# Compression matmuls of four weight tiles issued as one run of sixteen, and another pace of the side lanes

## The chip, the core and the metric

The kernel runs on one core of a Trainium2 chip. The metric is the device time of one launch in microseconds. The core's engines work side by side, each through its own queue of instructions in order: TensorE (PE: matmuls, with PEld for its weight loads), VectorE (DVE), ScalarE (ACT), GpSimd (POOL) and SyncE (SP), which here mostly issues DMAs.

## The reference

The reference is a trunk of two equal layers over 256 tokens of width 1024, in float32. A layer has a gated feed-forward block, three kinds of attention side by side whose results are gated and added, a second feed-forward block, and a gated addition of an embedding. The part that matters is the second kind of attention, `nsa_attention`. Its first branch compresses keys and values: windows of 32 tokens, 16 apart, are laid out as one row each, and a small network turns a row into one key or value.

```python
def compress(t, pos, w1, w2):
    c = t.reshape(bsz, n_chunk, B_CMP_STRIDE, B_GROUPS, B_HEAD_DIM)
    blk = jnp.concatenate([c[:, :-1], c[:, 1:]], axis=2) + pos[None, None, :, None, :]
    blk = blk.transpose(0, 1, 3, 2, 4).reshape(bsz, n_cmp, B_GROUPS, B_CMP_LEN * B_HEAD_DIM)
    return jax.nn.gelu(blk @ w1) @ w2
```

There are 15 windows and two groups, so `blk` has 30 rows of 2048, and `w1` is 2048x256, once for keys and once for values. The product `blk @ w1` is what the change is about. Its result goes through `gelu` and `w2` and is attended to by the same queries as the other two branches of `nsa_attention`.

## The kernel before, in words

Large products split each float32 operand into a high and a low part and add three matmuls (`mul3`, lines L265 to L267). Weights come through SP's queue as tiles of 128x1024 into `raw`; ScalarE copies the high part to `wh` (L258), VectorE subtracts it to get the low part `wl` (L253). There are six buffers of `wh` and six of `wl`. A product of 512 columns (`product`) walks the first 128 tokens through eight steps of the inner dimension and the second 128 tokens eight steps later, and calls `flow.tick()` after each three matmuls.

Attention is made of generators, the sides, that are stepped by these ticks. Side a (first attention), c (third) and b (second) share lane 0, one after the other; each has a pace, the steps that it takes for a tick of the main line (`PACE_A`, `PACE_B`, `PACE_C`, 0.8 each). The side `compressed` has lane 1 to itself at a pace of 1.0. The main line runs the projections A0, A1, A2, Ck, Cq, Bk, Bv, Bq, and then the gates and output products of the three branches in the order 0, 2, 1 (`gate` and `br`). Side a starts after A2, c and `compressed` after Bk, b after branch 0. Where a branch needs a side's result, the main line joins it: what is left of the side is stepped through at once.

The program is put in order by a list scheduler as it is built: on each engine it takes, of the instructions whose inputs are there, the one traced first. `tc.high_priority(offset=n)` makes an instruction count as traced n earlier, and `tc.keep_in_program_order` pins one behind the instruction traced before it on its engine. The scores of attention (`scores`, L1008) are written with both: twelve matmuls of 64 rows a group, of which eleven are ahead of other work and pinned to the one before, and the first is not.

The compression (`compressing`) holds its rows in `e` as 16 pieces of the inner dimension (k) for keys and for values (kv). One matmul takes 128 of the inner dimension, the 32 rows as the stationary operand, and 256 columns of `w1`. Each of four kinds, by kv and by k odd or even, writes another strip of 32 partitions of one PSUM bank, `c_ps` (`cmp` in the profile); a later matmul adds the strips. The weights `w1` are eight tiles of 128x1024 a layer (`Whole`, `w` in the profile), each for four matmuls; they are not split, and go by SP's queue straight into a buffer of `wh` or `wl`, in turn (L397). One is queued behind every second tile of the main line from Bv on. For each tile the loop waits until the tile and two queue places after it are fetched, `ready(j, 3)`, and issues its four matmuls (L1202). After the last, VectorE copies the bank to `c_sb` (L1205).

Of the kernel before, what the change touches and what calls it, by code (L numbers as in the profile page):

```python
# [43 lines left out]
LATE_ON = False  # L44
FLIPS = ["flip"]
POINTS = (5, 8, 11, 14, 18, 21)
PACE_A, PACE_B, PACE_C = 0.8, 0.8, 0.8

# [166 lines left out]
def trunk(ctx: ExitStack, tc: tile.TileContext, a: dict, out: bass.AP, index: list):  # L217
    nc = tc.nc
# [7 lines left out]
    def bank(tag, bufs, name):  # L226
        return psum.tile([128, 512], F32, tag=tag, bufs=bufs, name=name)
# [726 lines left out]
    def attention(i, norm, after):  # L954
# [215 lines left out]
        w1 = w2 = None  # L1170
# [10 lines left out]
        def compressing():  # L1181
            pos = pool.tile([128, 2, 2, 8], F32, name="pos")
            nc.sync.dma_start(pos, a["pos"][i].rearrange("p (v s j) -> p v s j", v=2, s=2))
            e = base.tile([128, 2, 2, 8, 32], F32, tag="blk", bufs=6, name="e")
            yield
            nc.vector.memset(e[:, :, 1, :, 31:32], 0.0)
            for kv in range(2):
                for s in range(2):
                    nc.vector.tensor_tensor(
                        e[:, kv, s, :, 0:32 - s],  # L1190
                        half[0][:, 2 * kv:2 * kv + 2, :].rearrange("p g (n j) -> p j (g n)", j=8)[:, :, s:],
                        pos[:, kv, s, :, None].to_broadcast([128, 8, 32 - s]), op=ALU.add)
                yield
            c_ps = bank("tp", 3, "cmp")
            for j in range(8):
                while not w1.ready(j, 3):
                    yield
                w = w1(j)
                for x in range(4):
                    k, kv = 2 * j + x // 2, x % 2  # L1200
                    q = 32 * (2 * (k % 2) + kv)
                    nc.tensor.matmul(c_ps[q:q + 32, :256], e[:, kv, k // 8, k % 8], w[:, 256 * x:256 * x + 256], start=j == 0, stop=j == 7)  # L1202
                yield
            c_sb[0] = pool.tile([128, 256], F32, name="c_sb")
            nc.vector.tensor_copy(c_sb[0], c_ps[:, :256])  # L1205

        def compressed():

            yield from compressing()
            yield  # L1210
            g_ps = tp_bank("gl")[:, :128]
# [320 lines left out]
        w1 = Whole(i, "w1")  # L1532
# [228 lines left out]
```

## Time and profile before

| | us |
|---|---|
| median of 3 runs | 1295.36 |
| lowest and highest | 1295.05 and 1295.36 |
| the profiled execution, time | 1295.46 |
| the profiled execution, span | 1293.7 |
| PE busy | 1283.7 |
| DVE busy | 1069.8 |
| ACT busy | 907.8 |

The span reaches from the first instruction's start to the last one's end; the execution's time has some 1.8 us around it. Attention takes some 250 us of each layer, from about 185 to 440 us in the first. Matmuls overlap in PE's pipeline, so the length of one, or a busy sum, says less than the distance between starts. A matmul of unsplit float32, as in the compression, stands in the profile as two records, and a merged row of the timeline counts records.

### The profile page before, as it was taken

The page shows a single profiled execution, that of the slowest core. Times are in us where ns is not written, and L with a number is a line of the kernel's source. Part 1 is how long each engine was busy: PE and PEld are TensorE (multiplying, and loading weights), DVE is VectorE, ACT ScalarE, POOL GpSimd, SP SyncE. Part 2 cuts the span into 40 slices and gives each one's busy share as a digit, 9 for nine tenths or more (in the row PEclk, how much of TensorE's full clock was granted, in tenths as well). Part 3 has the DMA queues.
Part 4 walks back from the last instruction along what each step waited for, and adds up shares of the span by engine and source line. Part 5 has one row for each costly group of instructions (what it writes and reads, how often), then busy time and mean ns, then how long its engine had stood idle before and what let it go on. Part 6 is the DMA issues. An engine that isn't in the chain of part 4 may idle for free.

```text
span 1293.7 us, 17861 instructions
## 1 busy us (share of the span) xinstructions
PE 1283.7 (99%) x6250; PEld 1052.7 (81%) x6250; DVE 1069.8 (83%) x1736; ACT 907.8 (70%) x1450; POOL 27.5 (2%) x46
## 2 busy tenths in 40 slices
PE   9999999999999999999999999999999999999997
PEld 7888888877878888888888888888778788888886
DVE  7878977666788799997799999777677978999975
ACT  6778667577587487876667876676765866787664
POOL 0000000000000000000000000000000000000000
PEclk9999999999999999999999999999999999999999
DMA  8778788465534568687666787865654435678772
GB/s 320 230 232 269 206 243 224 165 237 167 189 118 129 175 185 244 212 241 214 212 195 237 201 250 229 250 180 200 224 178 144 140 130 194 206 202 240 237 222 83
DMA packets 137179, 263.73 MB, mean 204 GB/s; under 512 B 71670, under 2 KB 77174, under 8 KB 137088
## 3 DMA queue, kind: packets, MB, share of 16 engines
q1 hardware_dynamic: 134128, 252.56, 63.4%
q0 software_dynamic: 2528, 9.47, 2.2%
q8 instruction: 49, 0.80, 0.3%
q10 hardware_dynamic: 432, 0.56, 0.1%
q14 instruction: 42, 0.34, 0.1%
HBM read 245.74 MB, written 1.08 MB: 191 GB/s over the span
## 4 chain that ended last, share of the span: by engine, by line
PE 99%; issue 0%; DVE 0%; ACT 0%; POOLq 0%; POOL 0%; DVEq 0%; ACTq 0%
PE ff L266 8%; PE ff L265 8%; PE ff L267 8%; PE fo L267 5%; PE fo L265 5%; PE fo L266 5%; PE p L265 4%; PE p L267 4%; PE p L266 4%; PE gate L265 4%; PE gate L266 4%; PE gate L267 4%; PE s L1008 2%; PE br L265 2%; PE A L266 2%; PE A L267 2%
## 5 line engine op out<-in xcount | busy, mean ns | idle before, releaser
L253 DVE TENSOR_TENSOR wl<-raw,wh 128x1024 fp32r<-128x1024 f32 (+1 forms) x410 | 491.8, 1213 | 85.2 <-ACT wh L258 84.2
L258 ACT ACTIVATE wh<-raw 128x1024 fp32r<-128x1024 f32 (+1 forms) x410 | 424.7, 1048 | 155.0 <-DMA raw<-in_wst 59.1
L266 PE MATMUL ff<-wl,nT 128*128 128x512 f32 x464 | 180.9, 390 | 0.0
L267 PE MATMUL ff<-wh,nT 128*128 128x512 f32 x464 | 180.3, 390 | 0.0
L265 PE MATMUL ff<-wh,nT 128*128 128x512 f32 x464 | 171.7, 390 | 0.0
L267 PE MATMUL fo<-wh,gT 128*128 128x512 f32 x304 | 117.1, 390 | 0.0
L266 PE MATMUL fo<-wl,gT 128*128 128x512 f32 x304 | 115.7, 389 | 0.0
L265 PE MATMUL fo<-wh,gT 128*128 128x512 f32 x304 | 114.3, 390 | 0.0
L266 PEld LDWEIGHTS ff<-wl,nT 128*128 128x128 f32 x464 | 87.1, 188 | 18.2 <-DVE wl L253 0.3
L265 PEld LDWEIGHTS ff<-wh,nT 128*128 128x128 f32 x464 | 87.1, 188 | 18.0
L267 PEld LDWEIGHTS ff<-wh,nT 128*128 128x128 f32 x464 | 87.1, 188 | 17.9
L265 PE MATMUL gate<-wh,nT 128*128 128x512 f32 x192 | 78.3, 408 | 0.0
L266 PE MATMUL gate<-wl,nT 128*128 128x512 f32 x192 | 76.8, 400 | 0.0
L267 PE MATMUL gate<-wh,nT 128*128 128x512 f32 x192 | 76.8, 402 | 0.0
L267 PEld LDWEIGHTS fo<-wh,gT 128*128 128x128 f32 x304 | 57.1, 188 | 11.8
L266 PEld LDWEIGHTS fo<-wl,gT 128*128 128x128 f32 x304 | 57.1, 188 | 11.8
L265 PEld LDWEIGHTS fo<-wh,gT 128*128 128x128 f32 x304 | 57.1, 188 | 11.7
L1021 ACT ACTIVATE p<-p,st 128x128 f32<-128x128 f32 (+1 forms) x128 | 56.6, 446 | 13.2 <-DVE st L1019 12.1
L606 ACT ACTIVATE whole<-flip 128x1024 uint16<-128x1024 uint16 x32 | 43.0, 1367 | 20.9 <-DMA flip<-cut 20.9
L600 ACT ACTIVATE cut<-gated 128x1024 uint16<-128x1024 uint16 (+1 forms) x48 | 46.3, 974 | 8.6 <-DVE gated L646 8.6
L253 DVE TENSOR_TENSOR wl<-x,wh 128x1024 fp32r<-128x1024 f32 x42 | 50.5, 1224 | 2.0 <-ACT wh L258 2.0
L258 ACT ACTIVATE wh<-x 128x1024 fp32r<-128x1024 f32 x42 | 43.8, 1049 | 5.7 <-DVE x L253 4.5
(391 smaller groups left out, 2734.0 us busy)
## 6 DMA issues: line engine op xcount, KB each, us to landing
raw<-in_wst SPq DMA_DIRECT2D x408, 512.0 KB, 4.4
w<-in_wst SPq DMA_DIRECT2D x16, 512.0 KB, 4.6
y<-in_wst POOLq DMA_DIRECT2D x6, 1024.0 KB, 6.6
band<-table SPq DMA_DIRECT2D x10, 512.0 KB, 4.7
xy<-in_wst POOLq DMA_DIRECT2D x4, 512.0 KB, 4.1
raw<-in_wbv SPq DMA_DIRECT2D x4, 420.0 KB, 3.1
xt<-in_xt SPq DMA_DIRECT2D x4, 256.0 KB, 5.5
raw<-in_wst SPq DMA_DIRECT2D x4, 256.0 KB, 5.2
```

The costliest lines, as they stand in the source:

```text
L253: nc.vector.tensor_tensor(o, x, y, op=ALU.subtract)
L258: nc.scalar.activation(hi, src, AF.Copy)
L265: nc.tensor.matmul(ps, xh, wh, start=start, stop=False, **kw)
L266: nc.tensor.matmul(ps, xh, wl, start=False, stop=False, **kw)
L267: nc.tensor.matmul(ps, xl, wh, start=False, stop=stop, **kw)
L600: nc.scalar.activation(cut.rearrange("p (w n) -> p w n", w=2), halves(src)[:, :128 * m].rearrange("p n w -> p w n"), AF.Copy)
L606: tc.keep_in_program_order(nc.vector.tensor_copy(to, of) if late else nc.scalar.activation(to, of, AF.Copy))
L1008: ins = nc.tensor.matmul(o, q[r, x, qb[m], t * 128:(t + 1) * 128], kk, start=x + y == 0, stop=x == 1)
L1021: nc.scalar.activation(p[j], p[j], AF.Exp, bias=st[:, j:j + 1], scale=-1.0, accum_out=st[:, n + j:n + j + 1])
```

## The change

The loop over eight tiles becomes a loop over two groups of four. It waits until the fourth tile of a group, and two queue places after it, are fetched, and then traces sixteen matmuls in the order of k and kv, so that each four in a row write the four strips. All but the first of a group count as traced 300 earlier and are pinned to the one before, as in `scores`. The terms of the sum are the same. Besides, `PACE_A` goes from 0.8 to 0.75, and `PACE_B` and `PACE_C` from 0.8 to 0.9.

```diff
-PACE_A, PACE_B, PACE_C = 0.8, 0.8, 0.8
+PACE_A, PACE_B, PACE_C = 0.75, 0.9, 0.9
...
             c_ps = bank("tp", 3, "cmp")
-            for j in range(8):
-                while not w1.ready(j, 3):
+            for b in range(0, 8, 4):
+                while not w1.ready(b + 4 - 1, 3):
                     yield
-                w = w1(j)
-                for x in range(4):
-                    k, kv = 2 * j + x // 2, x % 2
-                    q = 32 * (2 * (k % 2) + kv)
-                    nc.tensor.matmul(c_ps[q:q + 32, :256], e[:, kv, k // 8, k % 8], w[:, 256 * x:256 * x + 256], start=j == 0, stop=j == 7)
+                w = [w1(j) for j in range(b, b + 4)]
+                for k in range(2 * b, 2 * b + 2 * 4):
+                    for kv in range(2):
+                        q, o = 32 * (2 * (k % 2) + kv), 256 * (2 * (k % 2) + kv)
+                        with tc.high_priority(offset=300 if (k, kv) != (2 * b, 0) else 0):
+                            ins = nc.tensor.matmul(c_ps[q:q + 32, :256], e[:, kv, k // 8, k % 8], w[k // 2 - b][:, o:o + 256], start=k < 2, stop=k >= 14)
+                        if (k, kv) != (2 * b, 0):
+                            tc.keep_in_program_order(ins)
                 yield
```

## Prediction

> **What bounds the kernel now.** I read the page's busy shares first, then the chain that ended last, then the timeline of TensorE (PE) around the changed matmuls.
>
> ```profile
> span 1293.7 us, 17861 instructions
> PE 1283.7 (99%) x6250; PEld 1052.7 (81%) x6250; DVE 1069.8 (83%) x1736; ACT 907.8 (70%) x1450; POOL 27.5 (2%) x46
> PE 99%; issue 0%; DVE 0%; ACT 0%; POOLq 0%; POOL 0%; DVEq 0%; ACTq 0%
> L253 DVE TENSOR_TENSOR wl<-raw,wh 128x1024 fp32r<-128x1024 f32 (+1 forms) x410 | 491.8, 1213 | 85.2 <-ACT wh L258 84.2
> L258 ACT ACTIVATE wh<-raw 128x1024 fp32r<-128x1024 f32 (+1 forms) x410 | 424.7, 1048 | 155.0 <-DMA raw<-in_wst 59.1
> w<-in_wst SPq DMA_DIRECT2D x16, 512.0 KB, 4.6
> ```
>
> The last-ending chain is PE itself, 99%. Nothing else ends a wait that matters, so what counts is PE's issue time: the distance from one matmul's start to the next one's start. Durations overlap and cannot be added; starts can be subtracted. In the timeline rows below the first column is the start and the second the length of the merged group. A compression matmul is two records, so x2 is one matmul, x26 thirteen.
>
> ```profile
> 282.51 0.38 PE L273 MATMUL yt<-ident,yn 128*128 128x128 f32 x2
> 282.82 1.91 PE L1202 MATMUL cmp<-w,e 128*32 128x256 f32 x26
> 284.67 0.32 PE L1008 MATMUL s<-kC,qC 64*128 64x128 f32 x1
> 284.92 0.64 PE L1202 MATMUL cmp<-w,e 128*32 128x256 f32 x8
> 285.49 0.88 PE L1008 MATMUL s<-kC,qC 64*128 64x128 f32 x11
> 286.30 0.63 PE L1202 MATMUL cmp<-w,e 128*32 128x256 f32 x6
> 286.86 0.50 PE L265 MATMUL gate<-wh,nT 128*128 128x512 f32 x1
> ...
> 288.10 0.39 PE L267 MATMUL gate<-wh,nT 128*128 128x512 f32 x1
> 288.42 0.62 PE L1202 MATMUL cmp<-w,e 128*32 128x256 f32 x2
> 288.97 0.49 PE L265 MATMUL gate<-wh,nT 128*128 128x512 f32 x1
> ...
> 289.39 0.63 PE L1202 MATMUL cmp<-w,e 128*32 128x256 f32 x6
> 289.96 0.50 PE L265 MATMUL gate<-wh,nT 128*128 128x512 f32 x1
> 290.30 0.40 PE L266 MATMUL gate<-wl,nT 128*128 128x512 f32 x1
> ...
> 299.51 0.64 PE L1202 MATMUL cmp<-w,e 128*32 128x256 f32 x8
> 300.08 0.51 PE L1265 MATMUL yc<-pT,vC 128*128 128x512 f32 x1
> ...
> 308.06 0.63 PE L1202 MATMUL cmp<-w,e 128*32 128x256 f32 x6
> 308.62 0.50 PE L265 MATMUL gate<-wh,nT 128*128 128x512 f32 x1
> ...
> 312.71 0.62 PE L1202 MATMUL cmp<-w,e 128*32 128x256 f32 x2
> 313.26 0.50 PE L265 MATMUL gate<-wh,nT 128*128 128x512 f32 x1
> ```
>
> The reader is to see three things. First, the 32 matmuls of a layer run in eight scattered pieces (13, 4, 3, 1, 3, 4, 3, 1). Second, a piece costs the same whether it holds one matmul (288.42 to 288.97: 0.55 us), three (0.57) or four (299.51 to 300.08: 0.57), because four of them write four different 32-column strips and run together; thirteen (282.82 to 284.67) cost 1.85, four such rounds, so each further round costs (1.85-0.55)/3 = 0.43. Third, each piece pays at its borders. Two ordinary rows give the plain step:
>
> ```profile
> 303.63 0.40 PE L266 MATMUL br<-wl,yA 128*128 128x512 f32 x1
> 303.86 0.40 PE L267 MATMUL br<-wh,yA 128*128 128x512 f32 x1
> 304.19 0.98 PE L1008 MATMUL s<-kB,qB 64*128 64x256 f32 x12
> ```
>
> Full matmul to full matmul takes 0.23 us. Full to narrow takes 0.32 (288.10 to 288.42), 0.09 more; the first full matmul after a narrow one takes 0.34 (289.96 to 290.30), 0.11 more. A pair of borders costs 0.20.
>
> **What the compression costs before.** The five pieces after 288 cost 0.55+0.57+0.57+0.56+0.55 = 2.80, and five border pairs 1.00. The three pieces between 282.82 and 286.86 stand among twelve score matmuls, which would have paid the borders themselves. Those twelve alone take, at another place of the layer,
>
> ```profile
> 257.88 0.89 PE L1008 MATMUL s<-kC,qC 64*128 64x128 f32 x12
> 258.70 0.40 PE L265 MATMUL Bv<-wh,nT 128*128 128x280 f32 x1
> ```
>
> 0.82 us, so these three cost 4.04-0.82 = 3.22. Sum: 7.02 us a layer. The compression's busy time on PE is the same in both layers:
>
> ```profile
> 0.00:640.00 640.00, 6.33 (x64) 1.94 (x64) 0.42 (x1) 1.00 0.68 211
> 640.00:1294.00 654.00, 6.33 (x64) 1.94 (x64) 0.42 (x1) 0.99 0.64 197
> ```
>
> so 14.04 us in all.
>
> **The change, part by part.** *Sixteen in one run.* Sixteen matmuls are four full rounds; the piece of thirteen was three full rounds and one with a single matmul, so a whole run costs the same 1.85, and 2.05 with its borders. Two a layer: 4.10, against 7.02: 2.92 less a layer, 5.84 in all. The arithmetic, the weight loads and the copy of the sum out of PSUM are the same in number.
>
> *What keeps it from that.* Fifteen of the sixteen are put ahead of other work and pinned to the one before; the first is not. The scheduler takes a far later instruction when nothing earlier is ready: the row 304.19 is a score group of the second branch's side, which starts only after branch 0, while branch 0 is still in its first `br` product. The new second run is traced after its fourth tile is fetched, but its first matmul needs only tile 4 and can be taken as such a filler; the scattered single at 288.42 shows that place. Then tiles 4 and 5 follow at once (8 matmuls), tile 6 and tile 7 when they land. Tile 7 is issued late:
>
> ```profile
> 297.19 0.46 SPq L397 DMA_DIRECT2D w<-in_wst  x1
> ```
>
> and lands some 4.6 us on (the page's median for `w`), near 301.8. Pieces of 8, 4 and 4 would cost (0.55+0.43)+0.57+0.57+3×0.20 = 2.72 instead of 2.05: 0.67 less gain a layer. The first run has no such break: its tiles were there when thirteen and three of its matmuls ran at 282.82 and 284.92. So the second run's price lies between 2.05 and 2.72 (and, with a loose first matmul, higher still: a rival below). I take the middle, 0.33 a layer lost.
>
> *The score group in the first stretch.* Its first matmul at 284.67 stood apart from its eleven, and the compression sat between. With the compression gone from there a full matmul may take the place:
>
> ```profile
> 360.67 0.38 PE L1008 MATMUL s<-kB,qB 64*128 64x256 f32 x1
> 360.98 0.50 PE L266 MATMUL gate<-wl,nT 128*128 128x512 f32 x1
> 361.87 0.98 PE L1008 MATMUL s<-kB,qB 64*128 64x256 f32 x11
> ```
>
> Such a split costs 0.31 (360.67 to 360.98) and a border pair 0.20, 0.51 a layer; it takes place or not. I put down 0.2.
>
> *Waits and buffers.* No DMA is added; the sixteen `w` loads keep their place in SP's queue, so its order before the next weight loads is the same. The run holds two more `wh` and two more `wl` buffers of six for as long as tile 4 waits for tile 7, at most from 288 to about 312. Behind a late release stand ScalarE's `wh` copies and VectorE's `wl` subtractions for the next products. Cover: a gate product of four tiles gives its first tile free seven steps (21 full matmuls, 4.8 us) before the next product needs that buffer with four left, and copy and subtraction take 1.05 and 1.21 (1048 and 1213 ns in the page's groups). I take nothing; if the cover were gone, each layer would lose up to those 2.3 us. On PE's own queue everything stands behind a run's last four, should tile 7 land later than the scheduler thinks; one microsecond late is one lost, in each layer.
>
> *Pace.* By the code side a now takes a step at 0.75 of the main line's ticks, c and b at 0.9. This adds no instruction. It moves work of VectorE and ScalarE, which is off the path while PE is fed, and decides how many score groups split: seven of fourteen a layer now (rows of L1008 that hold x1; 284.67 and 360.67 are two of the first layer's), at 0.51 each. No row shows the other pace. One group more or less in each of two sides is ±1.0 a layer, ±2.0 in all; all fourteen split or none, ±7, are the far ends. I take zero, since the row gives no direction.
>
> **Sum.** 5.84 - 2×0.33 - 2×0.2 = 4.8 us less. The profiled execution took 1295.46 (span 1293.7), the median is 1295.36, so 1290.6.
>
> **Where the skill prices a piece by itself.** From the rows, a piece between full matmuls costs beside its rounds of 0.43 the border pair of 0.20 and 0.12 of filling inside (0.55-0.43): 0.32. The Trainium skill, TensorEngine Tiling (Array Packing), Key Properties, says that a change of tiling mode drains TensorE, whatever the modes are. The skill's TensorE: Matmul & The Clock Gate, Single matmul latency, puts what streaming hides of a matmul at 398 cycles of 2.4 GHz, 0.166 us; two such a piece, an estimate by that page, are 0.33, and by it six pieces and three rounds fewer a layer would give 3.27, or 1289.9 after my deductions. The trace agrees with it between full matmuls; whether it holds beside score groups is the first rival.
>
> **The rivals.**
>
> *Every piece is as dear (faster than the sum).* My 3.22 for the stretch with the scores holds three pieces, of which two border on scores; if six pieces less a layer brought 0.32 each, with 3 of 11 rounds less (3×0.43), a layer would save 3.21, and 2×3.21-1.06 = 5.4: 1290.0. Against it: the stretch, measured whole, came out at 3.22 with its six rounds (2.58), so its pieces cost 0.21 each. Chance 0.05.
>
> *The runs come apart (about no change).* Each first matmul is taken long before its fifteen (0.55+0.20 = 0.75 for it), and the second run's rest comes as tiles land (7, 4, 4: 2.72). A layer then pays 2.05+0.75+0.75+2.72 = 6.27, and a split score group 0.51: 0.24 saved, 0.5 in all: 1294.9. For it: seven score groups, pinned in the same way, split just so. Against it: the score group's halves write two banks, the compression one bank, whose operands are there at 282.82. Chance 0.11.
>
> *The faster side starves PE (slower).* Place: side b's softmax before the last joins, at pace 0.9. The first two rows are all work, the last two that on the tile `p` alone (PE, PEld, DVE, ACT):
>
> ```profile
> 360.00:380.00 20.00, 20.00 (x113) 15.32 (x112) 18.73 (x59) 16.34 (x46) 0.00 (x0) 1.00 0.50 159
> 380.00:400.00 20.00, 20.00 (x109) 15.61 (x108) 17.12 (x52) 18.58 (x47) 0.00 (x0) 1.00 0.35 106
> 360.00:380.00 20.00, 1.80 (x12) 1.46 (x12) 5.77 (x23) 8.72 (x34) 1.00 0.50 159
> 380.00:400.00 20.00, 3.32 (x20) 2.53 (x20) 5.89 (x18) 8.20 (x28) 1.00 0.35 106
> ```
>
> An eighth more of `p` a microsecond makes VectorE 18.73+0.72 = 19.5 of 20 in the first, ScalarE 18.58+1.03 = 19.6 in the second: just short. From 2.4 us of weight tiles late a layer on, the gain is gone; 3.7 a layer make it slower by 0.2%. With 4 a layer: 1298.6. Against it: the clock stands at 1.00 and PE has no gap in either row. Chance 0.08.
>
> *The pace joins score groups.* Two groups a layer fewer split, and both runs whole: 5.84+2.0, so 1287.5. Chance 0.07.
>
> **How the numbers follow.** My forecast, chance 0.69, runs from whole runs and one split group fewer a layer (1288.5) to pieces of 8, 4, 4 with the score group split and one more split (1295.4-5.84+1.34+1.02+1.02 = 1292.9). Change and no change part at 0.2%, 2.6 us, about what a measurement of this kernel can tell: 1292.8 and 1298.0. Faster: 0.67 of the forecast, 0.05 and 0.07, 0.79; same: 0.02+0.11, 0.13; slower 0.08. The range 1287.0 to 1294.5 leaves out the slower rival, half of the one that comes apart, and a little below.
>
> **What would show it.** Right: `cmp` in the timeline as x32, or as x16 with x8, over about 1.85 us each, four border pairs fewer to full matmuls; PE's chain still 99%. Wrong: groups of x2 before a gate matmul (the loose first); `gate`, `br` or `wo` matmuls that wait for `wl` or `wh`; fewer x12 score groups than seven a layer. If PE's idle time grows near 290 to 312, the held buffers did it; near 360 to 410, the pace.

## The result, and the profile after

The changed kernel takes 1287.54 us (median of four runs, 1286.75 to 1288.41) against 1295.36 before: a ratio of 0.9939, 95% interval 0.9921 to 0.9956. It is faster by 7.8 us, where 4.8 was forecast. The profiled execution took 1288.41, the upper end of its runs.

The page first, in the places that were read before: span, busy shares, and the chain that ended last.

```profile
span 1286.6 us, 17873 instructions
PE 1276.2 (99%) x6250; PEld 1051.1 (82%) x6250; DVE 1068.7 (83%) x1736; ACT 904.5 (70%) x1450; POOL 28.6 (2%) x46
PE 89%; DVE 4%; DMA 3%; ACT 2%; issue 2%; SPq 0%; POOL 0%; POOLq 0%; DVEq 0%; ACTq 0%
```

TensorE executes the same number of matmul records, 6250, and is still busy throughout; the other engines do what they did. The chain now passes through DMA, ScalarE and VectorE for a few per cent, which it did not before. The waits of the weight loads say where; the columns are the sum in us, how often, and the longest.

```profile
PEld ff L265 <- ACT wh L258: 1.2, 2, 0.7
PEld ff L266 <- DVE wl L253: 1.0, 2, 0.6
```

These are in the feed-forward blocks, which the change does not touch. The other runs of this kernel are up to 1.7 us shorter. A second profiled execution of it, of 1287.77 us (Experiment 2), has none of these four waits, and its chain is PE for 98%; it has a wait of another kind, shown in Experiment 5.

The timeline of TensorE around the compression, first layer (start, length of the merged group; two records are one compression matmul):

```profile
289.24 0.38 PE L1008 MATMUL s<-kC,qC 64*128 64x256 f32 x1
289.55 0.50 PE L265 MATMUL br<-wh,yA 128*128 128x512 f32 x1
...
291.12 0.97 PE L1008 MATMUL s<-kC,qC 64*128 64x256 f32 x11
292.03 0.44 PE L273 MATMUL yt<-ident,yn 128*128 128x128 f32 x2
...
294.13 1.93 PE L1203 MATMUL cmp<-w,e 128*32 128x256 f32 x32
295.99 0.55 PE L273 MATMUL pt<-ident,p 128*128 128x128 f32 x3
296.47 0.88 PE L1008 MATMUL s<-kC,qC 64*128 64x128 f32 x12
...
300.40 1.93 PE L1203 MATMUL cmp<-w,e 128*32 128x256 f32 x32
302.26 0.50 PE L1267 MATMUL yc<-pT,vC 128*128 128x512 f32 x1
302.69 0.98 PE L1008 MATMUL s<-kC,qC 64*128 64x256 f32 x12
```

Both runs are whole: 32 records without other work between them, 1.86 us each (294.13 to 295.99, 300.40 to 302.26). The second layer has the same two rows. The score groups at 296.47 and 302.69 are whole as well; only the one at 289.24 still has its first matmul apart. What remains of the compression's busy time on PE, one row a layer (the second column the stretch, the third PE):

```profile
0.00:640.00 640.00, 3.87 (x64) 1.87 (x64) 0.41 (x1) 1.00 0.69 213
640.00:1287.00 647.00, 3.89 (x64) 1.77 (x64) 0.42 (x1) 1.00 0.64 197
```

It was 6.33 a layer. Counted over both layers in the order of TensorE's instructions, the compression's 16 pieces are now 4, the 28 score groups that stood in 42 pieces stand in 36, and the stretches of narrow work between full matmuls are 40 instead of 50.

### The profile page after: what moved, and what is told of

Its sections match the earlier page's. It is cut to its first block, busy times and chain, and to the rows that moved or that the text cites. A ratio compares the mean times of both kernels' runs of the same rounds, so it can differ in the third digit from the quotient of the medians.

```text
span 1286.6 us, 17873 instructions
## 1 busy us (share of the span) xinstructions
PE 1276.2 (99%) x6250; PEld 1051.1 (82%) x6250; DVE 1068.7 (83%) x1736; ACT 904.5 (70%) x1450; POOL 28.6 (2%) x46
## 4 chain that ended last, share of the span: by engine, by line
PE 89%; DVE 4%; DMA 3%; ACT 2%; issue 2%; SPq 0%; POOL 0%; POOLq 0%; DVEq 0%; ACTq 0%
PE ff L266 6%; PE ff L265 6%; PE ff L267 6%; PE fo L267 5%; PE fo L265 5%; PE fo L266 5%; PE gate L266 4%; PE gate L267 3%; PE gate L265 3%; PE p L266 3%; PE p L267 3%; PE p L265 3%; DMA raw<-in_wst 3%; DVE wl L253 2%; PE s L1008 2%; PE br L265 2%
```

## The prices, and what the experiments were to tell apart

Theory "pieces": TensorE is fed all the time, so the time follows from what it has to issue. From the rows: 0.43 us for a round of compression matmuls and 0.12 for each piece, 0.20 for the borders of each narrow stretch; a score piece costs 0.31 with one matmul (289.24 to 289.55) and 0.9 with eleven or twelve (291.12 to 292.03), so 0.19 and about 0.12 for each two. These are scores of 256 columns; a group of 128 columns costs 0.82 (257.88 to 258.70 in the prediction), and the count takes no account of that. By these prices the narrow work of both layers comes to 50.9 us before and 43.0 after, 7.9 less. The rival theory, "pace", gives the runs the 5.8 us that the prediction worked out for whole runs, and the other 2 to the paces of the side lanes. The order of TensorE's instructions is known before a kernel runs, so each expectation is a count at these prices, taken from the 1295.4 before. The kernel before was measured again beside the experiments and came out between 1295.36 and 1295.88; each ratio is to the one on the same chip. "Ranked" below means that an instruction counts as traced earlier (`high_priority`).

| kernel | compression pieces a layer | score pieces, stretches (both layers) | count | measured median | ratio to before, 95% interval |
|---|---|---|---|---|---|
| before | 13, 4, 3, 1, 3, 4, 3, 1 | 42, 50 | | 1295.4 | |
| the change | 16, 16 | 36, 40 | 1287.5 | 1287.54 | 0.9939 (0.9921 to 0.9956) |
| runs alone | 16, 12, 4 | 36, 40 | 1287.5 | 1288.03 | 0.9946 (0.9934 to 0.9959) |
| pace alone | 10, 1, 13, 4, 4 | 42, 46 | 1293.0 | 1292.53 | 0.9980 (0.9971 to 0.9989) |
| runs of four | 12, 12, 4, 4 | 40, 46 | 1290.4 | 1290.27 | 0.9961 (0.9949 to 0.9974) |
| not pinned | 5, 2, 1, 2, 3, 3, 1, 8, 2, 1, 4 | 46, 58 | 1300.4 | 1299.01 | 1.0029 (1.0017 to 1.0040) |
| later bank first | 16, 16 | 34, 38 | 1286.5 | 1286.19 | 0.9924 (0.9911 to 0.9938) |
| one run of 32 | 32 | 42, 44 | 1289.7 | 1288.26 | 0.9942 (0.9930 to 0.9955) |
| first ranked too | 20, 8, 4 | 38, 44 | 1289.2 | 1290.64 | 0.9959 (0.9946 to 0.9971) |
| later bank, pace 1.0 | 16, 16 | 34, 38 | 1286.5 | 1286.70 | 0.9928 (0.9916 to 0.9940) |
| pace of a alone | 16, 16 | 36, 40 | 1287.5 | 1287.94 | 0.9943 (0.9931 to 0.9955) |

## Experiment 1: the runs without the paces, the paces without the runs

The runs alone:

```diff
-PACE_A, PACE_B, PACE_C = 0.75, 0.9, 0.9
+PACE_A, PACE_B, PACE_C = 0.8, 0.8, 0.8
```

> The runs of sixteen with the old paces (0.8 each). Theory 'pieces': the time is set by how many narrow pieces and border pairs TensorE has to issue (0.43 us a compression round, 0.12 a piece, 0.20 a border pair, 0.51 a split score group); the order that this kernel gets has 6 compression pieces and 36 score pieces in 40 narrow stretches, against 16, 42 and 50 before and 4, 36 and 40 with the whole change, so about 7.9 us less than before, 1287.5, the same as the whole change. Rival 'pace': the pace joined the score groups and brought some 2 us of the 7.8; then this kernel saves 5.8 or less, 1289.6 or above.

It took 1288.03. The trace of this kernel, first layer, the rows of L1203 and L1008 from 288 to 308 us:

```profile
288.91 1.93 PE L1203 MATMUL cmp<-w,e 128*32 128x256 f32 x32
291.69 0.98 PE L1008 MATMUL s<-kC,qC 64*128 64x256 f32 x12
296.00 1.50 PE L1203 MATMUL cmp<-w,e 128*32 128x256 f32 x24
304.45 0.64 PE L1203 MATMUL cmp<-w,e 128*32 128x256 f32 x8
305.02 0.62 PE L1008 MATMUL s<-kB,qB 64*128 64x256 f32 x5
306.00 0.62 PE L1008 MATMUL s<-kB,qB 64*128 64x256 f32 x5
307.82 0.38 PE L1008 MATMUL s<-kB,qB 64*128 64x256 f32 x2
```

With the old paces the second run does come apart, into twelve and four, as the prediction had feared; yet the gain is there, because the score pieces are down to 36 here too. So the runs, not the paces, took the score groups from 42 pieces to 36.

The paces alone are the kernel before with only the first line of the change, 0.75, 0.9 and 0.9.

> The old loop by tiles with the new paces. Theory 'pieces': 10 compression pieces and 42 score pieces in 46 stretches, by the same prices 2.4 us less than before, 1293.0; no score group is joined by the pace. Rival 'pace': the side work placed otherwise frees TensorE by itself, some 2 us through joined score groups, or the kernel gets slower where VectorE and ScalarE fill up between 360 and 400 us (1298 or more).

1292.53, 0.998 (0.9971 to 0.9989): the paces by themselves are worth 1.4 to 3.8 us by this interval, but only with the old loop. Its score pieces are 42 still; what the paces change is where the loose compression matmuls fall, 5 pieces a layer instead of 8. With the runs in place that is no longer to be had: the two gains do not add.

## Experiment 2: only side a's pace

```diff
-PACE_A, PACE_B, PACE_C = 0.75, 0.9, 0.9
+PACE_A, PACE_B, PACE_C = 0.75, 0.8, 0.8
```

> The runs of sixteen with only side a's pace changed (0.75, 0.8, 0.8). Theory 'pieces': the order has the same 4 compression pieces, 36 score pieces and 40 stretches as the whole change, so the same time, 1287.5; the paces of b and c bring nothing. Rival 'pace of b and c': they keep VectorE and ScalarE in time for the last join of side b; without them the kernel loses 1 us or more, 1288.5 and up.

> The whole change once more, to stand on the same chip as the two others of this call: 1287.5 by every theory.

1287.94 (1287.79 to 1289.05) beside 1287.77 (1287.03 to 1289.10) for the whole change on the same chip: no difference that can be seen. The paces of b and c bring nothing that shows here. Side a's pace makes the second run whole, but against the runs alone that too shows no difference: 1288.03 with 24 and 8 records.

## Experiment 3: the price of a piece, shorter runs

One tile's four matmuls to a run, ranked and pinned as before:

```diff
-            for b in range(0, 8, 4):
-                while not w1.ready(b + 4 - 1, 3):
+            for b in range(8):
+                while not w1.ready(b, 3):
...
-                w = [w1(j) for j in range(b, b + 4)]
-                for k in range(2 * b, 2 * b + 2 * 4):
+                w = [w1(b)]
+                for k in range(2 * b, 2 * b + 2):
```

> Whole change, but each run holds one tile's four matmuls, eight pinned runs a layer instead of two. Theory 'pieces': the runs stand in 8 pieces (12, 12, 4, 4 a layer) and 40 score pieces in 46 stretches: 5.0 us less than before, 1290.4. Rival 'rounds': the gain is in full rounds of four alone (no single matmuls in a round); these runs are full rounds too, so the whole gain stays, 1287.5.

1290.27, the count's 1290.4. All rounds are full here, and 2.7 us are lost all the same, in borders and in two score groups a layer that stand apart again. Rounds alone are not the gain.

## Experiment 4: sixteen matmuls without rank and pin

```diff
-                        with tc.high_priority(offset=300 if (k, kv) != (2 * b, 0) else 0):
-                            ins = nc.tensor.matmul(c_ps[q:q + 32, :256], ...)
-                        if (k, kv) != (2 * b, 0):
-                            tc.keep_in_program_order(ins)
+                        nc.tensor.matmul(c_ps[q:q + 32, :256], ...)
```

> Whole change without the pins and without the priority: four tiles are still waited for, the sixteen matmuls are free. Theory 'pieces': the order has 22 compression pieces and 46 score pieces in 58 stretches: 5.0 us more than before, 1300.4. Rival 'waiting for four tiles': what helps is that the sixteen are ready at one time; then this kernel keeps most of the gain, 1290 or below.

1299.01: slower than before, 1.0029 (1.0017 to 1.0040). The timeline of this kernel shows what sixteen matmuls that are ready together become when nothing holds them together:

```profile
293.77 1.05 PE L1202 MATMUL cmp<-w,e 128*32 128x256 f32 x10
295.01 0.63 PE L1202 MATMUL cmp<-w,e 128*32 128x256 f32 x4
295.83 0.62 PE L1202 MATMUL cmp<-w,e 128*32 128x256 f32 x2
296.64 0.63 PE L1202 MATMUL cmp<-w,e 128*32 128x256 f32 x4
297.19 0.32 PE L1008 MATMUL s<-kC,qC 64*128 64x128 f32 x1
297.44 0.63 PE L1202 MATMUL cmp<-w,e 128*32 128x256 f32 x6
298.01 0.89 PE L1008 MATMUL s<-kC,qC 64*128 64x128 f32 x11
299.41 0.63 PE L1202 MATMUL cmp<-w,e 128*32 128x256 f32 x6
302.69 0.62 PE L1202 MATMUL cmp<-w,e 128*32 128x256 f32 x2
303.67 1.07 PE L1202 MATMUL cmp<-w,e 128*32 128x256 f32 x16
304.67 0.38 PE L1008 MATMUL s<-kC,qC 64*128 64x256 f32 x1
```

Pieces of one, two and three matmuls at 0.55 to 0.56 each, with other work between them. Beside the paces alone (1292.53), waiting for four tiles without holding them together costs 6.5 us; rank and pin together turn that into a gain. Of the two it should be the rank: with only the pins taken away, the order on TensorE has the same pieces as that of the whole change, and with only the rank taken away nearly those of the kernel here (24 compression pieces in place of 22, and 46 score pieces). This was read from the two orders; neither was run.

## Experiment 5: the first matmul ranked too

```diff
-                        with tc.high_priority(offset=300 if (k, kv) != (2 * b, 0) else 0):
+                        with tc.high_priority(offset=300):
```

> Whole change, but the first matmul of each run counts as traced earlier too. Theory of the prediction ('loose first'): the first matmul at ordinary rank is what can come away from its run, so ranking it with the rest changes nothing or helps, 1287.5 or less. Theory 'pieces' by the order it gets: ranked early, a run starts before its later tiles are there and breaks as they land, 6 pieces (20, 8, 4 a layer) and 38 score pieces in 44 stretches, 6.2 us less than before, 1289.2.

1290.64: the loose first matmul is not the weakness that the prediction took it for. Left at ordinary rank it holds the run back until its last tile is nearly there. Ranked early, its first four matmuls follow the first run at once, the next eight come behind a few transposes, and the last four stand in PE's queue before tile 7 has landed:

```profile
293.80 2.37 PE L1203 MATMUL cmp<-w,e 128*32 128x256 f32 x40
...
296.68 1.07 PE L1203 MATMUL cmp<-w,e 128*32 128x256 f32 x16
...
300.24 0.40 PE L265 MATMUL br<-wh,yA 128*128 128x512 f32 x1
301.92 0.64 PE L1203 MATMUL cmp<-w,e 128*32 128x256 f32 x8 [1.28 <-DMA w<-in_wst]
```

The bracket is the idle time of PE before the row and what ended it: 1.28 us for the DMA of the tile. In the second layer the same wait is shorter:

```profile
936.26 0.64 PE L1203 MATMUL cmp<-w,e 128*32 128x256 f32 x8 [0.60 <-DMA w<-in_wst]
```

The count, 1289.2, has no waits in it; with these two it is 1291.1, half a microsecond above the median. The execution that shows them took 1289.80, though, 1.3 less than that, so the waits need not be what lifts the median over its count. In the changed kernel the same transfer is late as well, by less. In its first profiled execution PE does not wait for it, and the compression's weight loads do for a moment, in both layers together (us, times):

```profile
  DMA w<-in_wst: 0.5, 2
```

In its second profiled execution TensorE itself stands idle before the last four matmuls of the second run, 0.8 us over both layers:

```profile
302.07 0.64 PE L1203 MATMUL cmp<-w,e 128*32 128x256 f32 x8 [0.59 <-DMA w<-in_wst]
935.45 0.64 PE L1203 MATMUL cmp<-w,e 128*32 128x256 f32 x8 [0.21 <-DMA w<-in_wst]
```

Tile 7 was issued at 294.52 there and landed 7.5 us later, at 302.0; the prediction had taken the median of all tiles, 4.6. In the first execution this transfer took 6.6 us.

## Experiment 6: one run of thirty-two, and the buffers

```diff
-            for b in range(0, 8, 4):
-                while not w1.ready(b + 4 - 1, 3):
+            for b in range(0, 8, 8):
+                while not w1.ready(b + 8 - 1, 3):
...
-                w = [w1(j) for j in range(b, b + 4)]
-                for k in range(2 * b, 2 * b + 2 * 4):
+                w = [w1(j) for j in range(b, b + 8)]
+                for k in range(2 * b, 2 * b + 2 * 8):
```

> Whole change with one run of thirty-two a layer instead of two of sixteen: all eight tiles are held until it starts, four of six buffers of each kind. Theory 'pieces': 2 compression pieces, but 42 score pieces in 44 stretches, 5.7 us less than before, 1289.7, if the buffers have cover. Rival 'buffers': with two buffers left of each kind the weight copies come late and TensorE waits inside the gate products, several us a layer: 1295 or more, with gate matmuls waiting for wl in the waits.

1288.26, no slower than the count and 1.4 better, and not to be told from the whole change by the intervals of the table. The run is whole, and no gate product waits:

```profile
319.08 0.39 PE L1268 MATMUL yc<-pT,vC 128*128 128x512 f32 x1
319.40 3.66 PE L1203 MATMUL cmp<-w,e 128*32 128x256 f32 x64
322.99 0.50 PE L265 MATMUL br<-wh,yA 128*128 128x512 f32 x1
```

Four of six buffers of each kind are held until 319 us, and TensorE does not pay for it: in the first layer's attention no weight load waits for `wl` or `wh` but one each before a score group, 0.4 us, about what a weight load into a narrow stretch shows where it waited for nothing. So the prediction's nothing for two held buffers had cover to spare. The run saves a piece and loses it again, since the score groups fall to 42 pieces. The 1.4 us by which the count is too high are not settled; the profiled execution, the slowest of its five, took 1289.33, only 0.4 less than the count.

## Experiment 7: score groups that begin with the later bank

The score groups that still split cost 0.51 each. If a group's first matmul finds its PSUM bank free while the others wait for the group's second bank, beginning with the second should join it:

```diff
-                    for par in range(2):
+                    for par in (1, 0):
...
-                        with tc.high_priority(offset=0 if (m, x, y, par) == (0, 0, 0, 0) else 300):
+                        with tc.high_priority(offset=0 if (m, x, y, par) == (0, 0, 0, 1) else 300):
...
-                        if (m, x, y, par) != (0, 0, 0, 0):
+                        if (m, x, y, par) != (0, 0, 0, 1):
```

> Whole change; besides, a score group begins with the half that writes the second of its two banks, the one that softmax frees last. Theory 'second bank': a score group splits because its first matmul finds its bank free and the rest wait for the other bank; beginning with the later bank joins groups. The order has 34 score pieces in 38 stretches against 36 and 40: 1.0 us less than the whole change, some 1286.5. Rival: the splits come from the scheduler's filling of idle places alone, and the order of banks moves nothing measurable.

> The whole change with score groups that begin with the later bank, once more. Theory 'second bank' and 'pieces': two score groups fewer split in all, 1.0 us less than the whole change beside it, some 1286.5. Rival: what the first measurement showed, 1286.2 against 1287.5 in another call, was the difference of two calls; then no difference beside the whole change.

It took 1286.19 on one chip, where the whole change was not run beside it, and 1286.98 (1286.72 to 1288.01) on another, beside 1287.77 (1287.03 to 1289.10) for the whole change. The 0.8 us between those two are about the 1.0 of the count, but the intervals of the ratios, 0.9936 (0.9923 to 0.9948) and 0.9942 (0.9928 to 0.9955), overlap: a gain is likely, not proven. The trace shows the group that it joins. The whole change first, then this kernel:

```profile
381.68 0.38 PE L1008 MATMUL s<-kB,qB 64*128 64x256 f32 x1
...
382.42 0.97 PE L1008 MATMUL s<-kB,qB 64*128 64x256 f32 x11
```

```profile
383.11 0.97 PE L1008 MATMUL s<-kB,qB 64*128 64x256 f32 x12
```

It joins one group a layer of the four that split. That fits the second bank for this one, but does not prove it: in the whole change VectorE has read out both banks by 378.90, 2.8 us before the group's first matmul at 381.68, so on the chip nothing waited for a bank there, and it can have counted only when the order was made. For the other three the cause is open.

The same with the paces of b and c at 1.0:

> As the kernel that begins a score group with the later bank, and the paces of sides b and c at 1.0 instead of 0.9. Theory 'pieces': 33 score pieces in 37 stretches, 9.4 us less than before, 1286.0. Rival 'starved': at this pace VectorE and ScalarE are late with weight tiles between 360 and 400 us, and the time is 1289 or more.

1286.70: no starving, and no gain over 0.9 beside it either (1286.19). The expectation gave it half a microsecond for 33 score pieces in 37 stretches; the kernel that ran has 34 in 38, as with 0.9, and the table counts these.

## Why the prediction was right, and where it was not

*What bounds the kernel, and the price of a piece.* Right. That TensorE's issue time is the whole matter, that a round costs 0.43, a piece 0.12 more and a border pair 0.20, is what every count above is made of. Seven of the ten medians lie within 0.7 us of their count; that of the change itself was counted once its time was known, the others before they ran. Three are off by 1.4: the kernel with the first matmul ranked too, which is slower than counted and has waits that the count leaves out, and the unpinned one and that with one run of thirty-two, both faster than counted, for which no cause was found. The intervals of the ratios reach 1.2 to 2.3 us to each side, and every count lies inside its own but that of the one run of thirty-two, which lies just above. Taken from the kernel before on the same chip, that one is 7.6 us faster where 5.7 were counted.

*The time.* 1287.54 lies below all that the main forecast covers, 1288.5 to 1292.9, and where the last rival was put. The way and the price of the change were forecast rightly; that the time still falls into the stated range, 0.5 us above its lower end, is in part luck.

*A whole run costs what thirteen did.* Right: 1.86 us measured, 1.85 said.

*The second run in pieces, 0.33 a layer.* Wrong for this kernel: the run is whole. The step that failed is the filler argument. It is right that a first matmul of ordinary rank may be taken early, and with the old paces the second run did break, into twelve and four; here it stayed back long enough. Side a's pace decides it: the runs alone, with the second run broken, and the kernel of Experiment 2, with both whole, differ in nothing else. Why the pace does so is open.

*The score group in the first stretch, 0.2 a layer.* Nothing came of it. The group there came out whole (296.47), as the 5.84 had it before this deduction.

*The pace term, zero.* Right for the paces: with the runs in place they bring nothing that shows. But the score groups did change, from 42 pieces to 36, a gain of 6×0.51 = 3.1 us, of which the prediction had one group a layer in its stretch already; but the runs alone do that. The prediction looked for joined score groups in the paces only, and had no term for what the order of the compression does to the groups around it. How it does so is open: fewer pieces alone do not join groups, since the one run of thirty-two has the fewest and still 42 score pieces. That missing term, some 2 us, together with the 1.06 of deductions that did not come true, is the whole distance from 4.8 to 7.8.

*The last tile on PE's queue, zero.* Named rightly and put at nothing. In one of two profiled executions of the changed kernel it cost nothing on PE, in the other 0.59 and 0.21 us, since the transfer took 6.6 to 7.5 us and not 4.6. The sign that the prediction gave, idle time of PE near 290 to 312 for held buffers, would have misled here: what ends that idle time is the tile's own transfer. Another sign, a chain that is PE for 99%, holds in neither execution as it stands: 89% and 98%.

*The rivals.* The time fell where the last rival had put it, 1287.5, and its outcome is what the trace shows: both runs whole, and three split groups a layer fewer, one of which its 5.84 held already; its cause, the pace, is refuted by the runs alone. Runs that come apart all over were seen only with rank and pin taken away: then the kernel is slower than before, which is worse than that rival's 1294.9. The side that starves PE did not come. The two rows at the place where it was expected:

```profile
360.00:380.00 20.00, 20.00 (x112) 15.76 (x111) 18.80 (x61) 17.72 (x54) 0.00 (x0) 1.00 0.45 153
380.00:400.00 20.00, 20.00 (x117) 16.22 (x116) 17.26 (x48) 18.64 (x44) 0.00 (x0) 1.00 0.34 107
```

VectorE went from 18.73 to 18.80 and ScalarE from 18.58 to 18.64, not to 19.5 and 19.6: the quicker pace did not raise the work of these stretches, and why is not shown. The fullest stretch now lies earlier, where the rival did not look: from 300 to 320 ScalarE is busy for 19.81 of 20 us, where it had 13.14 before, and PE waits for nothing there in this execution.

```profile
300.00:320.00 20.00, 20.00 (x130) 15.36 (x129) 17.09 (x36) 19.81 (x45) 0.00 (x0) 1.00 0.70 228
```

*Every piece as dear.* The runs of four bear out the price between full matmuls: four more compression pieces and four more score pieces, in six more stretches, cost 2.7 us, where the count had 2.9. Beside score groups the border pair is not paid. The kernel with the paces alone has both cases:

```profile
290.71 0.38 PE L1008 MATMUL s<-kC,qC 64*128 64x256 f32 x1
291.02 0.62 PE L1202 MATMUL cmp<-w,e 128*32 128x256 f32 x2
291.57 0.97 PE L1008 MATMUL s<-kC,qC 64*128 64x256 f32 x11
...
298.65 0.33 PE L1008 MATMUL s<-kC,qC 64*128 64x128 f32 x1
298.91 0.50 PE L267 MATMUL br<-wh,yA 128*128 128x512 f32 x1
```

A single score matmul of 256 columns takes 0.31 before a compression piece (290.71 to 291.02), as before a full matmul (289.24 to 289.55), and a single compression matmul takes 0.55 between two score pieces (291.02 to 291.57), as between full ones. The 0.25 of the single score matmul in the unpinned kernel (297.19 to 297.44) is a matter of its 128 columns: before a full matmul that form takes 0.26 (298.65 to 298.91). So a piece pays its own price whatever stands beside it, and a change from one narrow form to another adds none of the 0.20. That is why the prediction's stretch among the scores came out at 0.21 a piece and not at 0.32: each of the three paid its 0.12, and the score group that they split 0.24 (0.25 and 0.81 against the 0.82 of a whole one). The Trainium skill, TensorEngine Tiling (Array Packing), Key Properties, has every change of tiling mode drain TensorE; the trace agrees between full and narrow, 0.09 and 0.11 us, and from one narrow form to another it shows no cost beyond the price that the piece pays anyway, in which a drain may be hidden.

## What to carry to other kernels

Where one engine is busy all the time, count what its order makes it issue: pieces, borders and rounds, each priced by a difference of two starts in the timeline. Such a count, read from the instruction order of a kernel not yet run, gave six of nine times here within 0.7 us, where the intervals reach 1.2 to 2.3 us to each side. And narrow matmuls that a scheduler may use as fillers should be ranked to stay together, but not so early that the last of them stands in the queue before its transfer has landed.

## What the runs showed that was not expected

Work that becomes ready together does not stay together: 16 matmuls collected and left free came out in eleven pieces a layer, where four at a time had made eight, and took 1299.01 against 1295.4. A change between two narrow forms costs TensorE none of the 0.20 us that a stretch pays toward full matmuls, though each piece still pays its own price. The last weight tile took up to 7.5 us to land, where the median of such tiles had been 4.6 before, and so in one execution TensorE waited inside a run that its order has whole. And holding all eight weight tiles, four of six buffers of each kind, until 319 us cost nothing that the waits show.
